# Separate load buffers for modulation chunks, their products three weight steps behind the load, and a written-out order on the load queue and on VectorE

## The chip, the core and the metric

The kernel runs on one core of a Trainium2 chip. The metric is device time in microseconds (us), the median of three runs. Engines are named as in the profile: PE is TensorE (PEld its weight loads), DVE is VectorE, ACT is ScalarE, POOL is GpSimd, and SP is the sync engine, which here does nothing but issue loads and stores.

## What is computed

Two layers of a diffusion transformer on 256 tokens of width 2048, in fp32. Layer 0 mixes tokens with a Hyena long convolution, layer 1 with a short gated convolution, and each ends in a SwiGLU feed-forward part of width 5632. Every sub-layer is modulated by vectors that come from one conditioning vector `c`:

```
m = silu(c) @ w_mod + b_mod            # six vectors of 2048 for each layer
sh1, sc1, g1, sh2, sc2, g2 = split(m)
a = rmsnorm(x, norm1_g) * (1 + sc1) + sh1
x = x + g1 * mixer(a)                  # hyena: w_in 2048x6144, w_out 2048x2048; short conv alike
a = rmsnorm(x, norm2_g) * (1 + sc2) + sh2
x = x + g2 * (silu(a @ w_gate) * (a @ w_up)) @ w_down
out = rmsnorm(x, final_g)
```

`w_mod` is 2 x 2048 x 12288 in fp32, some 200 MB of the 620 MB that the kernel reads. The rest are the weights of the matmuls.

## The kernel before

**Weights.** All matmul weights pass through one stream of 784 chunks of 128 x 1024 fp32 (512 KB). `emit_chunk(i)` loads chunk i into a tile `wraw`, and `split` makes two float32r tiles of it: ACT casts it to `whi` (L207), DVE subtracts that from the raw chunk and gives `wlo` (L208). `whi` and `wlo` have four buffers each. `lin` calls `next_chunk` once for two k tiles (one weight step); the chunks are emitted three steps ahead of the matmuls that use them (`LA = 3`). A step is 24 matmuls of 256 columns, or, where both parts of the activations lie side by side (`wide`), 8 of 512 columns (L258) and 8 of 256 (L262).

**Modulation.** The product `silu(c) @ w_mod` is not done on PE. Its weights come as 384 more chunks of 512 KB, tiles `mraw`; for each, one DVE instruction (L191) multiplies the chunk by the broadcast `cb` and sums along its rows into a column of `macc`. When a block of four k tiles is complete, `mod_finish` makes `mval` (L162, L163) and, for scales, `msc` (L166) of it. `mod_list` is the order of the chunks, `emit_mods(n)` takes the next n of them, each with its load and its product. Each segment of the program has a rate `mods`, in modulation chunks for each weight step, which `emit_chunk` adds up in `credit`: 0.9 in the hyena output and in the first feed-forward parts, 0.58 (`MF0`) in the rest of the feed-forward part of layer 0, 0.6 (`ML1`) in most of the short convolution, 0.2 in the last feed-forward part. `need_mods(l, m, kb)` takes as many as are missing before a modulation vector is read.

**Buffers and order.** `wraw` and `mraw` share one pool, `rawp`, of seven buffers. All loads are issued on SP, which takes them in order: a load whose buffer is not yet free holds up those behind it. The order of the instructions on each engine is not the order of the source: the program is built with a scheduler that simulates a timeline (`schedule_with_timeline_sim=True`) and places instructions by it. DVE, too, takes its instructions in that order and waits at the first one that isn't ready.

**Entries.** `Entry` begins a sub-layer before its norm is known: `prep` scales the residual and splits it (`xs`, `xsh`, `xsl`) and needs the shift vector for that, two groups of matmuls run on it, and then `make_a` makes the activations `ax`: DVE scales (`an`, L350), ACT adds the shift (L353), DVE gives the low part (L354). `make_a` needs both `msc` and `mval`. The layers' second norms have the keys `n2_0` and `n2_1`.

Of the kernel before, what the change touches and what calls it, by code (L numbers as in the profile page):

```python
# [11 lines left out]
F32 = mybir.dt.float32  # L12
# [3 lines left out]
ALU = mybir.AluOpType  # L16

P = 128
D = 2048
KT = D // P  # L20
T = 256
# [8 lines left out]
KD = 8  # L30
# [7 lines left out]
HT, HD, HI = 1, 1, 4  # L38
XW = T + 2

RSQRT_MAGIC = float(0x5F3759DF)
# [15 lines left out]


class Seg:
    def __init__(self, fn, chunks=(), mods=0.0):  # L60
# [4 lines left out]
def trunk_kernel(ctx: ExitStack, tc: tile.TileContext, A, out):  # L65
    nc = tc.nc

    cst = ctx.enter_context(tc.tile_pool(name="cst", bufs=1))
    rawp = ctx.enter_context(tc.tile_pool(name="rawp", bufs=7))
    hilo = ctx.enter_context(tc.tile_pool(name="hilo", bufs=4))  # L70
# [5 lines left out]
    def nm(s):  # L76
        uid[0] += 1
        return f"{s}_{uid[0]}"
# [12 lines left out]

# [1 line left out]
    crow = []  # L93
# [22 lines left out]
    def load_cols():  # L116
        nc.sync.dma_start(out=dcol, in_=A["k_dcol"])
        nc.sync.dma_start(out=vec, in_=A["vecs"])

    def V(name, i=0, n=1):  # L120
# [29 lines left out]

# [1 line left out]
    macc, mval, msc = {}, {}, {}  # L152
# [29 lines left out]

    def emit_mods(n):
        for _ in range(n):
            if mod_pos[0] >= len(mod_list):
                return
            l, m, kt, h, fin = mod_list[mod_pos[0]]
            mod_pos[0] += 1
            r = rawp.tile([P, 1024], F32, tag="raw", name=nm("mraw"))
            nc.sync.dma_start(out=r, in_=A["wm"][l, m, kt, h])  # L190
            nc.vector.scalar_tensor_tensor(  # L191
                out=r, in0=r, scalar=1.0, in1=cb[:, h * 1024:(h + 1) * 1024],
                op0=ALU.mult, op1=ALU.mult, accum_out=macc[l, m][:, kt, h:h + 1])
            if fin:
                mod_finish(l, m, *fin)

    def mods_through(n):
        emit_mods(max(0, n - mod_pos[0]))

    mod_end = {(e[0], e[1], e[2] // 4): i + 1 for i, e in enumerate(mod_list)}  # L200
# [3 lines left out]

# [1 line left out]
    def split(dst_hi, dst_lo, src):  # L206
        nc.scalar.copy(out=dst_hi, in_=src)  # L207
        nc.vector.tensor_tensor(out=dst_lo, in0=src, in1=dst_hi.bitcast(F32), op=ALU.subtract)  # L208

    stream, spos, semit, ready = [], [0], [0], {}  # L210
    LA = 3
    credit = [0.0]

    def emit_chunk(i):
        ap, mods = stream[i]
        r = rawp.tile([P, 1024], F32, tag="raw", name=nm("wraw"))
        nc.sync.dma_start(out=r, in_=ap)
        hi = hilo.tile([P, 1024], F32R, tag="hi", name=nm("whi"))
        lo = hilo.tile([P, 1024], F32R, tag="lo", name=nm("wlo"), bufs=NLO)
        split(hi, lo, r)  # L220
        ready[i] = (hi, lo)
        credit[0] += mods
        n = int(credit[0])
        credit[0] -= n
        emit_mods(n)
# [7 lines left out]
    def next_chunk():  # L233
        i = spos[0]
        spos[0] += 1
        while semit[0] < min(i + LA + 1, len(stream)):
            emit_chunk(semit[0])
            semit[0] += 1
        if bg:
            bg.pop(0)()  # L240
        return ready.pop(i)
# [21 lines left out]

# [1 line left out]
    def rsqrt_steps(v, y, a, b):  # L265
# [15 lines left out]
    def rstd_from(parts):  # L281
        # parts: tiles [P, n, T] of squares, summed over partitions with tokens on partitions
        p = ps("pss")
        for h in range(2):
            cols = [t[:, j, h * P:(h + 1) * P] for t in parts for j in range(t.shape[1])]
            for i, c in enumerate(cols):
                nc.tensor.matmul(p[:, h:h + 1], c, ones[:, 0:1], start=(i == 0), stop=(i == len(cols) - 1))
        return rstd_of([p[:, 0:2]])
# [40 lines left out]
    def pairs(n, name):  # L329
        # [part, k tile, hi/lo, token]: both parts of a k tile lie side by side  # L330
        ts = [S([P, 2, 2, T], F32R, name) for _ in range(n // 2)]
# [24 lines left out]

# [1 line left out]
    def sin_layer(w, rhs, bcol, n):  # L358
# [102 lines left out]

    def a_task(kb):
        make_a(acts0, kb, x0[kb], st0["r"], 0, True)

# [18 lines left out]

# [1 line left out]
    segs = []  # L485
# [3 lines left out]

# [1 line left out]
    a0 = acts0  # L491
# [168 lines left out]
    class Entry:  # L660
# [44 lines left out]
        def group(self, i, order):  # L705
            # groups 0 and 1 over the first KD k tiles, before the statistics are known
            flush_bg()
# [134 lines left out]

# [1 line left out]
    e1 = Entry(1, True, "n1_1")  # L844
# [71 lines left out]
    def tail_close(pss):  # L916
        # the last four feature tiles enter the sum of squares one by one
        p = acc_box["tail"]
# [31 lines left out]

# [1 line left out]
def _chunks(w):  # L952
# [80 lines left out]
```

## Time and profile before

| | us |
|---|---|
| median of 3 runs | 2444.77 (2442.78 to 2445.31) |
| span of the profiled execution, first to last instruction | 2440.7 |
| median less that span | 4.1 |
| PE busy in the span | 2363.8 |
| DVE busy | 1848.5 |
| ACT busy | 1119.7 |

The profiled execution is known by its span alone; the 4.1 us are the difference of two executions and are taken as what lies around the span. A matmul counts as busy from its start to a modelled end, so PE's share says little: how many matmuls start in a stretch is the better measure. A waiting engine is shown with what released it.

### The profile page before, as it was taken

How to read it: one execution, taken by the hardware profiler on the slowest of the kernel's cores; microseconds unless marked ns; L12 is line 12 of the kernel's file. 1: busy time of each engine (PE TensorE's matmuls, PEld its weight loads, DVE VectorE, ACT ScalarE, POOL GpSimd, SP SyncE). 2: the span in 40 equal slices, each digit the busy share in tenths (PEclk: the TensorE clock that was granted, in tenths of full speed). 3: DMA queues.
4: the chain of work that ended last, by engine and by line, in shares of the span. 5: the costliest groups of instructions: out<-in, count | busy, mean ns of one | idle time of the engine just before them, and what ended most of it. 6: DMA issues, size and time to landing. Idle time of an engine off the chain costs nothing.

```text
span 2440.7 us, 38816 instructions
## 1 busy us (share of the span) xinstructions
PE 2363.8 (97%) x15040; PEld 2111.2 (87%) x15040; DVE 1848.5 (76%) x2729; ACT 1119.7 (46%) x1527; POOL 83.2 (3%) x94
## 2 busy tenths in 40 slices
PE   7899999999999999999999999999999999999998
PEld 3699998999998888888789888879988888888887
DVE  7979999898887777777777988778766656655554
ACT  3445444454544333444345444435545433444543
POOL 5000111010000000000000000001000000000000
PEclk9899999999999999999999999999999999999998
DMA  7899776889888888888876888886777677755662
GB/s 268 319 333 329 244 225 209 293 316 333 314 283 276 281 283 278 273 289 278 275 260 195 300 306 285 273 264 222 234 220 228 222 221 228 232 184 188 186 185 95
DMA packets 172525, 624.24 MB, mean 256 GB/s; under 512 B 19533, under 2 KB 19886, under 8 KB 172340
## 3 DMA queue, kind: packets, MB, share of 16 engines
q1 hardware_dynamic: 172340, 621.77, 76.5%
q8 instruction: 117, 1.92, 0.3%
q14 instruction: 68, 0.56, 0.1%
HBM read 619.59 MB, written 2.10 MB: 255 GB/s over the span
## 4 chain that ended last, share of the span: by engine, by line
PE 70%; DMA 14%; DVE 10%; issue 4%; POOL 1%; ACT 0%; DVEq 0%; SPq 0%; ACTq 0%; POOLq 0%
PE ps L258 26%; PE ps L262 23%; DMA mraw<-in_wm 14%; PE ps L261 9%; PE ps L260 9%; DVE wlo L208 4%; DVE mraw L191 3%; DVE xres L753 1%; DVE fy L368 0%; POOL rs L277 0%; DVE cg L342 0%; PE pz L616 0%; PE pz L615 0%; PE pz L617 0%; PE pU L583 0%
## 5 line engine op out<-in xcount | busy, mean ns | idle before, releaser
L207 ACT CAST whi<-wraw 128x1024 fp32r<-128x1024 f32 x784 | 816.3, 1049 | 932.0 <-PE ps L258 625.3
L208 DVE TENSOR_TENSOR wlo<-wraw,whi 128x1024 fp32r<-128x1024 f32 x784 | 950.3, 1220 | 298.8 <-ACT whi L207 298.1
L262 PE MATMUL ps<-ax,wlo 128*128 128x256 f32 x4160 | 1138.5, 283 | 15.0 <-DVE wlo L208 14.6
L258 PE MATMUL ps<-ax,whi 128*128 128x512 f32 x2688 | 945.6, 398 | 0.0
L262 PEld LDWEIGHTS ps<-ax,wlo 128*128 128x128 f32 x4160 | 780.7, 191 | 27.6 <-DVE wlo L208 23.6
L191 DVE SCALAR_TENSOR_TENSOR mraw<-mraw,cb 128x1024 f32<-128x1024 f32 x384 | 477.6, 1246 | 245.8 <-DMA mraw<-in_wm 245.5
L258 PEld LDWEIGHTS ps<-ax,whi 128*128 128x128 f32 x2688 | 504.0, 188 | 118.6
L258 PE MATMUL ps<-hx,whi 128*128 128x512 f32 x1328 | 468.2, 397 | 0.0
L261 PE MATMUL ps<-ax,whi 128*128 128x256 f32 x1472 | 409.7, 285 | 1.8 <-DVE ax L354 1.8
L260 PE MATMUL ps<-ax,whi 128*128 128x256 f32 x1472 | 404.0, 285 | 7.5 <-ACT whi L207 5.7
L262 PE MATMUL ps<-hx,wlo 128*128 128x256 f32 x1408 | 397.2, 282 | 9.5 <-DVE wlo L208 9.3
L258 PEld LDWEIGHTS ps<-hx,whi 128*128 128x128 f32 x1328 | 249.3, 188 | 59.6
L260 PEld LDWEIGHTS ps<-ax,whi 128*128 128x128 f32 x1472 | 281.7, 194 | 8.8 <-ACT whi L207 6.5
L261 PEld LDWEIGHTS ps<-ax,whi 128*128 128x128 f32 x1472 | 284.9, 194 | 2.3 <-DVE ax L354 2.0
L262 PEld LDWEIGHTS ps<-hx,wlo 128*128 128x128 f32 x1408 | 266.2, 189 | 14.7 <-DVE wlo L208 14.4
L262 PE MATMUL ps<-zx,wlo 128*128 128x256 f32 x512 | 143.0, 284 | 6.2 <-DVE wlo L208 5.9
L262 PEld LDWEIGHTS ps<-zx,wlo 128*128 128x128 f32 x512 | 96.5, 190 | 9.6 <-DVE wlo L208 9.6
L341 ACT COPY fb<-ps 128x256 f32<-128x256 f32 x168 | 61.8, 369 | 91.5 <-DVE cg L342 59.8
L258 PE MATMUL ps<-zx,whi 128*128 128x512 f32 x256 | 90.9, 398 | 0.0
L753 DVE SCALAR_TENSOR_TENSOR xres<-ps,mval,xres 128x256 f32<-128x256 f32 x168 | 72.4, 476 | 12.3 <-PE ps L262 12.1
L260 PE MATMUL ps<-zx,whi 128*128 128x256 f32 x256 | 71.2, 283 | 0.7 <-DVE z L619 0.7
L261 PE MATMUL ps<-zx,whi 128*128 128x256 f32 x256 | 71.7, 283 | 0.0
(153 smaller groups left out, 1598.5 us busy)
## 6 DMA issues: line engine op xcount, KB each, us to landing
mraw<-in_wm SPq DMA_DIRECT2D x384, 512.0 KB, 4.7
wraw<-in_wgu SPq DMA_DIRECT2D x352, 512.0 KB, 4.5
wraw<-in_wd SPq DMA_DIRECT2D x176, 512.0 KB, 4.3
wraw<-in_hw_in SPq DMA_DIRECT2D x96, 512.0 KB, 5.0
wraw<-in_sw_in SPq DMA_DIRECT2D x96, 512.0 KB, 4.4
wraw<-in_hw_out SPq DMA_DIRECT2D x32, 512.0 KB, 5.0
wraw<-in_sw_out SPq DMA_DIRECT2D x32, 512.0 KB, 4.4
xin<-in_xT SPq DMA_DIRECT2D x4, 512.0 KB
```

Of the source, the lines that this page charges most:

```text
L191: nc.vector.scalar_tensor_tensor(out=r, in0=r, scalar=1.0, in1=cb[:, h * 1024:(h + 1) * 1024], op0=ALU.mult, op1=ALU.mult, accum_out=macc[ ...
L207: nc.scalar.copy(out=dst_hi, in_=src)
L208: nc.vector.tensor_tensor(out=dst_lo, in0=src, in1=dst_hi.bitcast(F32), op=ALU.subtract)
L258: nc.tensor.matmul(pss[n], wh, both, start=st, stop=False)
L260: nc.tensor.matmul(o, wh, xh, start=st, stop=False)
L261: nc.tensor.matmul(o, wh, xl, start=False, stop=False)
L262: nc.tensor.matmul(o, wl, xh, start=False, stop=sp)
L341: nc.scalar.copy(out=b, in_=p[:, T:2 * T])
L753: nc.vector.scalar_tensor_tensor(out=xa, in0=pss[n][:, c * T:(c + 1) * T], scalar=mval[l, gate][:, kt:kt + 1], in1=xa, op0=ALU.mult, op1=A ...
```

## The change

The pool `rawp` has five buffers instead of seven and holds weight chunks (and one table, `draw`). A new pool `mrawp` has five buffers for modulation chunks. The load of a modulation chunk and its product are parted: `load_mods` issues the load and puts the product into a list `mq`; `drain_mods` takes products off it that are three calls of `next_chunk` old (`MLAG`), and a full list (five) or a `need_mods` takes them earlier. `emit_chunk` first issues the loads of chunks up to i + 2 (`RL`) and then splits chunk i. `chain` ties each instruction that it is given to the one before it with the same key, without a semaphore: it fixes their order for the scheduler. There is one such chain of all `wraw` and `mraw` loads on SP, and one of all `wlo` subtractions and modulation products on DVE. What else is on DVE is still placed by the scheduler. `a_task` asks for its modulation vectors itself. The program reserves less memory for dynamic DMA (`dynamic_dma_scratch_size=1024`), and some comments are gone.

```diff
+RAWB, MRAWB, MLAG, RL = 5, 5, 3, 2
+NOSYNC = mybir.DependencyInfo(mybir.DependencyClass.NoSync, mybir.DependencyReason.DATA)
-    rawp = ctx.enter_context(tc.tile_pool(name="rawp", bufs=7))
+    rawp = ctx.enter_context(tc.tile_pool(name="rawp", bufs=RAWB))
+    mrawp = ctx.enter_context(tc.tile_pool(name="mrawp", bufs=MRAWB))
+    def chain(key, ins):
+        p = last.get(key)
+        if p is not None:
+            tc.add_manual_dep(ins.ins, p.ins.name, NOSYNC, reason="chain")
+        last[key] = ins
+        return ins
-    def emit_mods(n):
+    def run_mod(r, l, m, kt, h, fin):
+        chain("dve", nc.vector.scalar_tensor_tensor(
+            out=r, in0=r, scalar=1.0, in1=cb[:, h * 1024:(h + 1) * 1024],
+            op0=ALU.mult, op1=ALU.mult, accum_out=macc[l, m][:, kt, h:h + 1]))
+        if fin:
+            mod_finish(l, m, *fin)
+    def drain_mods(upto):
+        while mq and mq[0][0] <= upto:
+            mq.pop(0)[1]()
+    def load_mods(n):
         for _ in range(n):
             if mod_pos[0] >= len(mod_list):
                 return
-            l, m, kt, h, fin = mod_list[mod_pos[0]]
+            e = mod_list[mod_pos[0]]
             mod_pos[0] += 1
-            r = rawp.tile([P, 1024], F32, tag="raw", name=nm("mraw"))
-            nc.sync.dma_start(out=r, in_=A["wm"][l, m, kt, h])
-            nc.vector.scalar_tensor_tensor(
-                out=r, in0=r, scalar=1.0, in1=cb[:, h * 1024:(h + 1) * 1024],
-                op0=ALU.mult, op1=ALU.mult, accum_out=macc[l, m][:, kt, h:h + 1])
-            if fin:
-                mod_finish(l, m, *fin)
+            if len(mq) >= MRAWB:
+                mq.pop(0)[1]()
+            r = mrawp.tile([P, 1024], F32, tag="mraw", name=nm("mraw"))
+            chain("sp", nc.sync.dma_start(out=r, in_=A["wm"][e[0], e[1], e[2], e[3]]))
+            mq.append((mtick[0], lambda r=r, e=e: run_mod(r, *e)))
+    def emit_mods(n):
+        load_mods(n)
     def mods_through(n):
         emit_mods(max(0, n - mod_pos[0]))
+        while mod_pos[0] - len(mq) < n:
+            mq.pop(0)[1]()
+    def load_raw(i):
+        r = rawp.tile([P, 1024], F32, tag="raw", name=nm("wraw"))
+        chain("sp", nc.sync.dma_start(out=r, in_=stream[i][0]))
+        raws[i] = r
     def emit_chunk(i):
-        ap, mods = stream[i]
-        r = rawp.tile([P, 1024], F32, tag="raw", name=nm("wraw"))
-        nc.sync.dma_start(out=r, in_=ap)
+        mods = stream[i][1]
+        while lpos[0] < min(i + RL + 1, len(stream)):
+            load_raw(lpos[0])
+            lpos[0] += 1
+        r = raws.pop(i)
...
-        split(hi, lo, r)
+        chain("dve", split(hi, lo, r))
...
             emit_chunk(semit[0])
             semit[0] += 1
+            mtick[0] += 1
+            drain_mods(mtick[0] - MLAG)
...
     def a_task(kb):
+        need_mods(0, 0, kb)
         make_a(acts0, kb, x0[kb], st0["r"], 0, True)
...
-    nc = bacc.Bacc("TRN2", target_bir_lowering=False, num_devices=1)
+    nc = bacc.Bacc("TRN2", target_bir_lowering=False, num_devices=1, dynamic_dma_scratch_size=1024)
```

What this does to the order of the instructions is shown at three places. A name's last number counts the tiles in the source's order, so a load and its reader carry the same number.

The first place is the feed-forward part of layer 0, in the down projection. On SP before, the loads stand in this order:

```order
L217 DMA wraw_10080<-in_wd 128x1024
L190 DMA mraw_10086<-in_wm 128x1024
L217 DMA wraw_10105<-in_wd 128x1024
L217 DMA wraw_10127<-in_wd 128x1024
L190 DMA mraw_10133<-in_wm 128x1024
L217 DMA wraw_10152<-in_wd 128x1024
L190 DMA mraw_10158<-in_wm 128x1024
```

On DVE before, the readers of these loads stand like this:

```order
L208 TENSOR_TENSOR wlo_10061<-wraw_10058,whi_10060 128x1024
L191 SCALAR_TENSOR_TENSOR mraw_10158,macc_1_123<-mraw_10158,cb 128x1024
L208 TENSOR_TENSOR wlo_10083<-wraw_10080,whi_10082 128x1024
L208 TENSOR_TENSOR wlo_10108<-wraw_10105,whi_10107 128x1024
L191 SCALAR_TENSOR_TENSOR mraw_10217,macc_1_123<-mraw_10217,cb 128x1024
L208 TENSOR_TENSOR wlo_10130<-wraw_10127,whi_10129 128x1024
L208 TENSOR_TENSOR wlo_10155<-wraw_10152,whi_10154 128x1024
```

The product of `mraw_10158` stands ahead of the splits of four weight chunks (10080, 10105, 10127, 10152) that are loaded before it. Over the whole feed-forward part of layer 0, every product stands four splits ahead in this way (five in one case).

The loads of the same part on SP now:

```order
L249 DMA wraw_10016<-in_wd 128x1024
L249 DMA wraw_10039<-in_wd 128x1024
L220 DMA mraw_10045<-in_wm 128x1024
L249 DMA wraw_10064<-in_wd 128x1024
L249 DMA wraw_10086<-in_wd 128x1024
L220 DMA mraw_10092<-in_wm 128x1024
```

And their readers on DVE now:

```order
L239 TENSOR_TENSOR wlo_10067<-wraw_10016,whi_10066 128x1024
L239 TENSOR_TENSOR wlo_10089<-wraw_10039,whi_10088 128x1024
L201 SCALAR_TENSOR_TENSOR mraw_10045,macc_1_126<-mraw_10045,cb 128x1024
L239 TENSOR_TENSOR wlo_10114<-wraw_10064,whi_10113 128x1024
L239 TENSOR_TENSOR wlo_10136<-wraw_10086,whi_10135 128x1024
L201 SCALAR_TENSOR_TENSOR mraw_10092,macc_1_126<-mraw_10092,cb 128x1024
```

Now the readers stand in the order of the loads; so it is everywhere but at 17 products at the end of the hyena output, at the entry `n2_1` and in the first down projection of layer 1, which stand one or two splits ahead.

The second place is the end of the hyena output, where `prep` of `n2_0` takes the modulation chunks that are missing. DVE before, from one split to the third after it:

```order
L208 TENSOR_TENSOR wlo_5564<-wraw_5561,whi_5563 128x1024
L678 COPY xs_5570<-mval_3_115 128x3x2
L191 SCALAR_TENSOR_TENSOR mraw_5615,macc_3_114<-mraw_5615,cb 128x1024
L319 TENSOR_TENSOR sqh_5554<-sq_5552 128x512
L191 SCALAR_TENSOR_TENSOR mraw_5618,macc_3_114<-mraw_5618,cb 128x1024
L191 SCALAR_TENSOR_TENSOR mraw_5621,macc_3_114<-mraw_5621,cb 128x1024
L208 TENSOR_TENSOR wlo_5606<-wraw_5603,whi_5605 128x1024
L208 TENSOR_TENSOR xsl_5576<-xs_5570,xsh_5575 128x774
L324 TENSOR_TENSOR ssacc_4987<-ssacc_4987,sqh_5554 128x512
L191 SCALAR_TENSOR_TENSOR mraw_5624,macc_3_114<-mraw_5624,cb 128x1024
L208 TENSOR_TENSOR wlo_5665<-wraw_5662,whi_5664 128x1024
```

DVE now, in the same weight step, up to the next split (two products, `mraw_5517` and `mraw_5569`, and `sqh_5556` stand just ahead of the first row, behind `wlo_5611`):

```order
L177 TENSOR_TENSOR mval_4_120<-macc_4_119 128x4
L239 TENSOR_TENSOR xsl_5581<-xs_5575,xsh_5580 128x774
L201 SCALAR_TENSOR_TENSOR mraw_5614,macc_3_117<-mraw_5614,cb 128x1024
L366 TENSOR_TENSOR ssacc_4993<-ssacc_4993,sqh_5556 128x512
L178 TENSOR_TENSOR mval_4_120<-mval_4_120,vec 128x4
L201 SCALAR_TENSOR_TENSOR mraw_5617,macc_3_117<-mraw_5617,cb 128x1024
L201 SCALAR_TENSOR_TENSOR mraw_5619,macc_3_117<-mraw_5619,cb 128x1024
L181 SCALAR_TENSOR_TENSOR msc_4_121<-mval_4_120,vec 128x4
L201 SCALAR_TENSOR_TENSOR mraw_5621,macc_3_117<-mraw_5621,cb 128x1024
L201 SCALAR_TENSOR_TENSOR mraw_5624,macc_3_117<-mraw_5624,cb 128x1024
L201 SCALAR_TENSOR_TENSOR mraw_5627,macc_3_117<-mraw_5627,cb 128x1024
L239 TENSOR_TENSOR wlo_5672<-wraw_5563,whi_5671 128x1024
```

Between two splits there were at most three products; now there are eight in a row, with `sqh`, `xsl` and `ssacc` among them, before `wlo_5672`.

The third place is the entry `n2_1`, where the first two activation blocks are made. The activations of k tiles 12 and 13 are `ax_17685` before and `ax_17692` now; chunk 530 of the stream (counted from 0) is multiplied by them. On DVE before, they stand behind split 530 (`wlo_17763`):

```order
L208 TENSOR_TENSOR wlo_17714<-wraw_17711,whi_17713 128x1024
L354 SCALAR_TENSOR_TENSOR ax_17683<-an_17720,mval_3_129,ax_17683 128x256
L354 SCALAR_TENSOR_TENSOR ax_17683<-an_17724,mval_3_129,ax_17683 128x256
L354 SCALAR_TENSOR_TENSOR ax_17684<-an_17728,mval_3_129,ax_17684 128x256
L354 SCALAR_TENSOR_TENSOR ax_17684<-an_17732,mval_3_129,ax_17684 128x256
L208 TENSOR_TENSOR wlo_17763<-wraw_17760,whi_17762 128x1024
L354 SCALAR_TENSOR_TENSOR ax_17685<-an_17780,mval_3_129,ax_17685 128x256
```

Now the last five products of the shift vector and four `an` stand behind split 530 (`wlo_17769`), and the rows that follow are these (`wlo_17938` is split 533):

```order
L201 SCALAR_TENSOR_TENSOR mraw_17778,macc_3_131<-mraw_17778,cb 128x1024
L392 SCALAR_TENSOR_TENSOR an_17799<-xres_4645,msc_4_135,rstd_17684 128x256
L392 SCALAR_TENSOR_TENSOR an_17849<-xres_4639,msc_4_135,rstd_17684 128x256
L392 SCALAR_TENSOR_TENSOR an_17853<-xres_4639,msc_4_135,rstd_17684 128x256
L239 TENSOR_TENSOR wlo_17846<-wraw_17718,whi_17845 128x1024
L239 TENSOR_TENSOR wlo_17892<-wraw_17766,whi_17891 128x1024
L239 TENSOR_TENSOR wlo_17938<-wraw_17843,whi_17937 128x1024
L177 TENSOR_TENSOR mval_3_132<-macc_3_131 128x4
L178 TENSOR_TENSOR mval_3_132<-mval_3_132,vec 128x4
L396 SCALAR_TENSOR_TENSOR ax_17692<-an_17787,mval_3_132,ax_17692 128x256
```

The activations that chunk 530 needs moved from behind split 530 to behind split 533, and split 533 needs the buffer of chunk 529.

## Rows read from the trace of the kernel before

**Rows 1.** The page: span, and busy time of each engine.
```profile
span 2440.7 us, 38816 instructions
...
PE 2363.8 (97%) x15040; PEld 2111.2 (87%) x15040; DVE 1848.5 (76%) x2729; ACT 1119.7 (46%) x1527; POOL 83.2 (3%) x94
```

**Rows 2.** Stretches: from:to, length, busy us (count) per engine, clock, DMA share, GB/s.
```profile
120.00:240.00 120.00, 120.00 (x1002) 120.00 (x1002) 103.23 (x157) 60.52 (x85) 0.00 (x0) 1.00 0.93 330
...
480.00:520.00 40.00, 40.00 (x335) 40.00 (x335) 38.07 (x61) 20.46 (x25) 0.00 (x0) 1.00 0.97 353
...
780.00:1260.00 480.00, 461.53 (x2576) 394.88 (x2575) 352.86 (x513) 199.29 (x244) 0.00 (x0) 1.00 0.84 279
1520.00:1660.00 140.00, 132.70 (x732) 111.65 (x732) 106.74 (x162) 58.06 (x73) 0.00 (x0) 1.00 0.81 266
...
1800.00:2340.00 540.00, 540.00 (x3058) 468.20 (x3057) 319.05 (x402) 244.33 (x311) 0.00 (x0) 1.00 0.67 211
```

**Rows 3.** Waits in 780 to 1260: total us, times, longest us.
```profile
DVE mraw L191 <- DMA mraw<-in_wm: 126.8, 80, 3.5
...
PE ps L262 <- DVE wlo L208: 18.1, 26, 1.8
```

**Rows 4.** DVE in order of time, 1103 to 1110: start, us, what, idle before.
```profile
1103.37 1.23 DVE L191 SCALAR_TENSOR_TENSOR mraw<-mraw,cb 128x1024 f32<-128x1024 f32 x1 [0.73 <-DMA mraw<-in_wm]
...
1104.52 2.36 DVE L208 TENSOR_TENSOR wlo<-wraw,whi 128x1024 fp32r<-128x1024 f32 x2
1109.43 1.22 DVE L191 SCALAR_TENSOR_TENSOR mraw<-mraw,cb 128x1024 f32<-128x1024 f32 x1 [2.56 <-DMA mraw<-in_wm]
```

**Rows 5.** SP in order of time, the load for that second product.
```profile
1104.63 0.33 SPq L190 DMA_DIRECT2D mraw<-in_wm  x1
```

**Rows 6.** The page's costliest groups: the two halves of a split.
```profile
L207 ACT CAST whi<-wraw 128x1024 fp32r<-128x1024 f32 x784 | 816.3, 1049 | 932.0 <-PE ps L258 625.3
L208 DVE TENSOR_TENSOR wlo<-wraw,whi 128x1024 fp32r<-128x1024 f32 x784 | 950.3, 1220 | 298.8 <-ACT whi L207 298.1
```

**Rows 7.** DVE in order of time, late in the hyena input (369 to 392).
```profile
369.64 2.35 DVE L208 TENSOR_TENSOR wlo<-wraw,whi 128x1024 fp32r<-128x1024 f32 x2
371.91 0.68 DVE L594 TENSOR_TENSOR ym<-pU,Kspec 128x512 f32<-128x512 f32 x1
...
377.49 2.31 DVE L191 SCALAR_TENSOR_TENSOR mraw<-mraw,cb 128x1024 f32<-128x1024 f32 x1
...
391.52 1.21 DVE L208 TENSOR_TENSOR wlo<-wraw,whi 128x1024 fp32r<-128x1024 f32 x1
```

**Rows 8.** PE in order of time, its waits at 392 and 441.
```profile
392.79 0.39 PE L262 MATMUL ps<-ax,wlo 128*128 128x256 f32 x1 [3.54 <-DVE wlo L208]
...
441.39 0.74 PE L617 MATMUL pz<-mh,Yl 128*128 128x256 f32 x4 [1.65 <-DVE Yl L208]
442.87 0.38 PE L260 MATMUL ps<-zx,whi 128*128 128x256 f32 x1 [0.74 <-DVE z L619]
```

**Rows 9.** Two stretches of 10 us around 400, columns as in rows 2.
```profile
390.00:400.00 10.00, 7.21 (x48) 7.21 (x49) 10.00 (x15) 2.23 (x3) 0.66 (x1) 0.83 0.59 172
400.00:410.00 10.00, 10.00 (x87) 10.00 (x86) 8.85 (x15) 5.51 (x9) 0.00 (x0) 1.00 0.90 315
```

**Rows 10.** DVE and then PE in order of time, entry n2_0.
```profile
541.89 1.27 DVE L350 SCALAR_TENSOR_TENSOR an<-xres,msc,rstd 128x256 f32<-128x256 f32 x3
...
544.22 1.22 DVE L191 SCALAR_TENSOR_TENSOR mraw<-mraw,cb 128x1024 f32<-128x1024 f32 x1
...
545.89 0.39 PE L261 MATMUL ps<-ax,whi 128*128 128x256 f32 x1 [1.77 <-DVE ax L354]
```

**Rows 11.** DVE at startup, first and last of ten products in a row.
```profile
75.22 1.21 DVE L191 SCALAR_TENSOR_TENSOR mraw<-mraw,cb 128x1024 f32<-128x1024 f32 x1
...
85.75 1.21 DVE L191 SCALAR_TENSOR_TENSOR mraw<-mraw,cb 128x1024 f32<-128x1024 f32 x1
```

**Rows 12.** The page's DMA issues: count, KB each, median us to landing.
```profile
mraw<-in_wm SPq DMA_DIRECT2D x384, 512.0 KB, 4.7
```

More of the change, by code (lines that the diff above doesn't have):

```diff
@@ L118, in load_cols @@
         nc.sync.dma_start(out=vec, in_=A["vecs"])
+    last = {}
+    def chain(key, ins):
[4 more added lines that the diff above has]
+        return ins
     def V(name, i=0, n=1):
@@ L181, in trunk_kernel @@
     mod_pos = [0]
-    def emit_mods(n):
+    mq, mtick = [], [0]
+    def run_mod(r, l, m, kt, h, fin):
[8 more added lines that the diff above has]
+    def load_mods(n):
         for _ in range(n):
@@ L207, in split @@
         nc.scalar.copy(out=dst_hi, in_=src)
-        nc.vector.tensor_tensor(out=dst_lo, in0=src, in1=dst_hi.bitcast(F32), op=ALU.subtract)
+        return nc.vector.tensor_tensor(out=dst_lo, in0=src, in1=dst_hi.bitcast(F32), op=ALU.subtract)
     stream, spos, semit, ready = [], [0], [0], {}
@@ L212, in trunk_kernel @@
     credit = [0.0]
-    def emit_chunk(i):
-        ap, mods = stream[i]
-        r = rawp.tile([P, 1024], F32, tag="raw", name=nm("wraw"))
-        nc.sync.dma_start(out=r, in_=ap)
+    raws, lpos = {}, [0]
+    def load_raw(i):
+        r = rawp.tile([P, 1024], F32, tag="raw", name=nm("wraw"))
+        chain("sp", nc.sync.dma_start(out=r, in_=stream[i][0]))
+        raws[i] = r
+    def emit_chunk(i):
+        mods = stream[i][1]
[3 more added lines that the diff above has]
+        r = raws.pop(i)
         hi = hilo.tile([P, 1024], F32R, tag="hi", name=nm("whi"))
         lo = hilo.tile([P, 1024], F32R, tag="lo", name=nm("wlo"), bufs=NLO)
-        split(hi, lo, r)
+        chain("dve", split(hi, lo, r))
         ready[i] = (hi, lo)
```

## The prediction

> **What bounds the kernel now.** First the page's first lines: PE counts as busy for 2363.8 of 2440.7 us [rows 1]. Since a busy PE is not PE at its peak, I then cut the span into stretches and counted the matmuls that start in each. Where only 256-column matmuls run, 1002 start in 120 us, 0.1198 us each; where wide steps run undisturbed, 3058 start in 540 us, 0.1766 each in their mix [rows 2]. A weight step is thus 24 x 0.1198 = 2.88 us narrow, or 16 x 0.1766 = 2.83 us wide. Most of the span runs at that pace and can give nothing. Two wide stretches don't: 780 to 1260, the bulk of layer 0's feed-forward part, has 2576 matmuls, worth 2576 x 0.1766 = 454.9 us, in 480, so 25.1 us are lost; 1520 to 1660, the short convolution, has 732, worth 129.3 in 140, so 10.7 are lost [rows 2]. The clock is full in both. PE's own waits there come to only 18.1 us in 26 pieces; the rest of the loss hides in the modelled ends of matmuls.
>
> Next, who is late in 780 to 1260: PE waits for `wlo` and DVE waits for loads of `mraw`, 126.8 us in 80 waits [rows 3]. The order of instructions (the first place above) says how: a product stands four splits ahead of weights that were loaded before it. DVE in order of time shows one round. The product at 1103.37 ends at 1104.60, splits follow, and the next product starts at 1109.43 after 2.56 us of waiting [rows 4]. Its load was issued at 1104.63, just as the earlier product had ended [rows 5], 4.8 us before its use; a load of `mraw` takes 4.7 us in the median [rows 12]. So each product frees the buffer that the next product's load needs, DVE sits out a whole trip of a load, and the splits behind the waiting product come late for PE. It is not lack of bandwidth as such: the DMA share is 0.84 at 279 GB/s, while 480 to 520 shows 353 GB/s with PE at its own pace, 335 x 0.1198 = 40.1 us in 40 [rows 2].
>
> **The change part by part.** The sum is made against the profiled execution, 2440.7, plus the 4.1 us by which the median lies above it [rows 1].
>
> *Feed-forward part of layer 0.* With products in load order and five weight buffers, weight load j can be issued when split j-5 is done, and the `mraw` load behind it at the same time, since its own five buffers are freed far earlier. Both are then about five steps, 5 x 2.83 = 14.1 us, ahead of their readers; three times the 4.7 us of a trip. DVE has 352.86 us of work for 454.9 us of PE [rows 2, 3]; 78%, so it keeps up if the pieces come evenly: between two splits stands at most one product, 1.2 + 1.2 us in 2.83. The traffic would be 279 x 480/454.9 = 294 GB/s, below the 353 shown. Bounds: 0 to -25.1. I take **-25.1**, being nearest to the undisturbed stretch.
>
> *Short convolution.* The same pattern (products four splits ahead) and the same bounds, 0 to -10.7; 266 x 140/129.3 = 288 GB/s. I take **-10.7**.
>
> *Hyena input.* Between the splits at 369.64 and 391.52 DVE has some 19 us of other work, among it three products, one of 2.31 us [rows 7] and two of 1.2. PE waits 3.54 us for the late split at 392.79 [rows 8] and then runs at a granted clock of 0.83: 48 matmuls in 7.21 us where 48 x 0.1198 = 5.75 would do, 1.5 lost [rows 9]. In the new order these three products stand elsewhere, 4.7 us less before the split, which covers the 3.54. Both losses go: **-5** (0 to -8; beyond -5 if the waits around it shrink too). Just behind it PE waits 1.65 for `Yl` and 0.74 for `z` [rows 8]; `Yl` stands earlier now: **-2** (0 to -3).
>
> *End of the hyena output, `n2_0`.* This is the second place. PE's cover: a split can start when the step four before it has freed its `hi`/`lo` buffers, and its halves take 1.05 + 1.22 = 2.3 us [rows 6]; so what stands between two splits, the later split's own 1.2 included, is hidden up to 4 x 2.88 - 2.3 = 9.2 us. There stand eight products at 1.15 = 9.2 us (ten in a row at startup start 1.17 apart [rows 11]), `sqh` and `ssacc` at about 0.6 each (`ym` of that width 0.68 [rows 7]) and `xsl` about 0.9 (between `ym` and a product by its width), 11.5 with small change, 12.7 with the split. Stall 3.5, and behind a stall of that length a stretch at reduced clock as after the 3.54 above, 1.5. One product, 1.22 us, leaves the chain at 544.22 ahead of PE's wait of 1.77 [rows 10]: -1.2. Net **+4** (0 if the scheduler's order leaves `hi`/`lo` slack that I don't see; 8 if the loads of these eight, for five buffers, come late too). Queued behind the products is `wlo_5672`, for which only PE waits.
>
> *Entry `n2_1`.* The third place. The activations for chunk 530 now stand behind split 533. That split needs the buffer of chunk 529, so PE finishes 529 and then has nothing until split 533 and the `ax` rows are through: ACT's and DVE's halves 2.3, then `mval`, the `ax` of k tile 12 (0.42 each, as `an` [rows 10]) with ACT's adds between. But DVE itself comes late: five products 5.8, four `an` 1.7, three splits 3.6 stand in the row, 11 us before `mval`. I take a wait of 5 and 1.5 of clock: **+6.5** (3, the bare chain behind 529, to 9, with DVE's row half uncovered).
>
> *Startup.* Ten products come 1.17 us apart [rows 11]: by the buffers, five allow a round of 4.7 + 1.15 = 5.9 us, 1.17 each, just the present pace. By bandwidth 0.524 MB at 353 GB/s is 1.49 us [rows 2]. So **+1** (-0.5 to +2). *At no cost:* a cluster of six products in the first down projection of layer 1, 6.9 us, lies under the cover of 4 x 2.83 - 2.3 = 9.0 (gone, the excess over it would show on PE); the reserved DMA memory issues nothing; the ties carry no semaphore.
>
> Sum: -25.1 - 10.7 - 5 - 2 + 4 + 6.5 + 1 = -31.3; 2440.7 - 31.3 + 4.1 = 2413.5, forecast **2414 us**.
>
> **A rule against it.** [Rows 2] show 353 GB/s in 480 to 520, in loads of 512 KB. The Trainium skill, "DMA: Bandwidth & Descriptors", section "Measured (HBM→SBUF, 128 partitions, SWDGE, issued from GpSimd)", asks to batch transfers to 1 MiB or more for three quarters of the peak and lists 341 GB/s at 1 MB; by it 512 KB loads would be near their limit, and an earlier issue would buy little: rival 3's time. The trace disagrees, by those 353 GB/s.
>
> **Rivals.** 1. *The two entries don't stall:* what I count as late in the written order is covered by slack on ACT and PE. For it: covers of 9 us exist; against it: the present order has waits of 3.54 and 1.77 at lighter places [rows 8, 10]. Without +4 and +6.5, 2403 us. 2. *Half of the feed-forward gain:* DVE at 78% becomes the pacer, since pieces of `swiglu` and of the norm fall between split and product, which are now bound to one order. 25.1 + 10.7 half recovered: 2414 + 18 = 2432. 3. *The loads are at their limit, slower:* if the mix of weights and modulation can't be had faster than the 279 GB/s of 780 to 1260, the loss there moves from "product waits" to "split waits" and nothing of 35.8 comes back, while the entries and startup still cost 11.5 and the hyena gives 7: 2444.8 + 4.5 = 2449. It decides from the point where less than 4.5 of 35.8 us are recovered, that is if the stretch stays below some 282 GB/s (an eighth of the way from 279 to 294, and a little). Against it: 353, and 330 over 120 to 240 [rows 2]. 4. *It doesn't do what it says:* PE's lost time there has another source, since its waits for `wlo` are only 18.1 of 25.1 us [rows 3], and the clumps cost less than I think: about 2445.
>
> **How the numbers follow.** Forecast with its sizes 58%, its own range 2405 to 2423; rival 1 17%; rival 2 14%; rival 3 6%; rival 4 5%. A measurement of this kernel tells some 0.2%, 4.9 us, from no change. The first three cases all lie below 2440: faster 0.89; rival 4 gives same 0.05; rival 3 slower 0.06. The range 2399 to 2435 holds the first three down to a rival 1 with 4 us more of hyena and up to a rival 2 with 3 us less; left out are rivals 3 and 4, 11%, and the tails of the others, some 6%.
>
> **What would show it.** Right: the feed-forward stretch with about 342 matmuls for each 60 us (60/0.1766 = 340) and DMA near 294 GB/s; DVE's waits for `mraw` there from 126.8 us to a few; the 3.54 before the hyena's convolution gone; new PE waits of about 3.5 us behind `wlo_5672` and 5 us for `ax` at `n2_1`. Wrong: DVE waiting for `wraw` instead at an unchanged rate (rival 3); PE waits for `wlo` while DVE is never idle (rival 2); no new waits at the entries (rival 1); startup longer by more than 2 us.

## The result, and the profile after

The changed kernel takes **2405.28 us** (median; 2404.43 to 2406.43) against 2445.04 for the kernel before, run beside it: a ratio of 0.9842, 95% interval 0.9828 to 0.9856. The forecast was 2414 with a range of 2399 to 2435. The profiled execution has a span of 2402.6, 2.7 below the median; the span fell by 38.1 us.

The top of the page of the changed kernel, to be read against [rows 1]:

```profile
span 2402.6 us, 38382 instructions
...
PE 2344.8 (98%) x15040; PEld 2107.5 (88%) x15040; DVE 1851.5 (77%) x2729; ACT 1125.3 (47%) x1527; POOL 75.1 (3%) x94
...
mraw<-in_wm SPq DMA_DIRECT2D x384, 512.0 KB, 5.5
```

Each engine has as many working instructions as before, and a load of `mraw` takes longer to land, 5.5 us against 4.7 [rows 12]. So no load became faster; what went is waiting. Stretches of the changed kernel, columns as in [rows 2]:

```profile
505.00:515.00 10.00, 6.76 (x44) 6.55 (x44) 9.41 (x15) 3.48 (x4) 0.00 (x0) 0.83 0.99 362
...
1660.00:1670.00 10.00, 4.04 (x34) 3.84 (x32) 10.00 (x17) 2.10 (x2) 0.00 (x0) 0.83 0.32 93
1670.00:1680.00 10.00, 8.86 (x53) 8.86 (x54) 9.39 (x22) 7.31 (x21) 0.00 (x0) 0.66 0.47 190
...
780.00:1260.00 480.00, 480.00 (x2719) 416.19 (x2718) 372.78 (x534) 215.71 (x261) 0.00 (x0) 1.00 0.84 288
```

In 780 to 1260 now 2719 matmuls start, 0.1765 us each: PE's own pace, as forecast (480 / 0.1766 = 2718, or 340 in 60 us; the 342 beside it in the prediction is a slip). The three longest waits there:

```profile
ACT whi L238 <- PE ps L300: 250.8, 164, 1.8
DVE wlo L239 <- ACT whi L238: 98.7, 117, 1.6
DVE xres L796 <- PE ps L304: 7.2, 7, 1.4
```

The 126.8 us of DVE waiting for `mraw` [rows 3] have no row any more. DVE waits for ACT, and ACT for PE to free a `whi` buffer: PE sets the pace. DVE in order of time shows the same place as [rows 4]:

```profile
1101.27 1.22 DVE L201 SCALAR_TENSOR_TENSOR mraw<-mraw,cb 128x1024 f32<-128x1024 f32 x1
...
1102.95 1.23 DVE L239 TENSOR_TENSOR wlo<-wraw,whi 128x1024 fp32r<-128x1024 f32 x1 [0.46 <-ACT whi L238]
1105.82 1.23 DVE L239 TENSOR_TENSOR wlo<-wraw,whi 128x1024 fp32r<-128x1024 f32 x1 [1.64 <-ACT whi L238]
1106.96 1.22 DVE L201 SCALAR_TENSOR_TENSOR mraw<-mraw,cb 128x1024 f32<-128x1024 f32 x1
```

No product carries a wait. The two stalls that were forecast stand in the trace. First the clump at the end of the hyena output, the eight products in a row, on DVE (the rows between are left out):

```profile
495.15 1.21 DVE L239 TENSOR_TENSOR wlo<-wraw,whi 128x1024 fp32r<-128x1024 f32 x1
496.29 1.22 DVE L201 SCALAR_TENSOR_TENSOR mraw<-mraw,cb 128x1024 f32<-128x1024 f32 x1
...
505.46 1.22 DVE L201 SCALAR_TENSOR_TENSOR mraw<-mraw,cb 128x1024 f32<-128x1024 f32 x1
...
507.24 1.23 DVE L201 SCALAR_TENSOR_TENSOR mraw<-mraw,cb 128x1024 f32<-128x1024 f32 x1 [0.56 <-DMA mraw<-in_wm]
...
508.39 3.49 DVE L239 TENSOR_TENSOR wlo<-wraw,whi 128x1024 fp32r<-128x1024 f32 x3
```

and PE behind it:

```profile
509.66 0.58 PE L304 MATMUL ps<-zx,wlo 128*128 128x256 f32 x1 [3.24 <-DVE wlo L239]
```

From 496.29 to the end of the late split some 13 us, as worked out; PE waits 3.24. Then the entry `n2_1`, on DVE:

```profile
1659.48 1.22 DVE L201 SCALAR_TENSOR_TENSOR mraw<-mraw,cb 128x1024 f32<-128x1024 f32 x1
...
1664.46 1.22 DVE L201 SCALAR_TENSOR_TENSOR mraw<-mraw,cb 128x1024 f32<-128x1024 f32 x1
...
1666.80 3.49 DVE L239 TENSOR_TENSOR wlo<-wraw,whi 128x1024 fp32r<-128x1024 f32 x3
1670.20 0.15 DVE L177 TENSOR_TENSOR mval<-macc 128x4 f32<-128x4 f32 x1
```

and on PE, which waits for the activation that needs that `mval`:

```profile
1671.14 1.23 PE L302 MATMUL ps<-ax,whi 128*128 128x256 f32 x4 [7.10 <-ACT ax L395]
```

Where the time went is seen best by setting the start of the n-th matmul of one trace against that of the other (both issue 15040, in nearly the same order; worked out from the starts in the traces, us):

```
n-th matmul   before    after   after - before   what lies since the row above
 1200          220.1    221.7    +1.6            startup
 3200          480.4    476.5    -3.9            hyena input, its convolution
 3600          528.4    529.4    +1.0            clump at n2_0
 4000          581.4    577.5    -3.9            entry n2_0
 5600          782.5    779.2    -3.3            first part of layer 0's feed-forward
 8400         1301.7   1273.1   -28.6            the rest of it
 9600         1491.7   1462.2   -29.5
10700         1689.7   1649.1   -40.6            short convolution and its output
10800         1703.7   1661.2   -42.4            a wait for rdiag at n2_1 that is gone
11200         1764.8   1732.4   -32.4            entry n2_1
12800         2047.5   2015.0   -32.4
14800         2399.3   2361.3   -38.1            down projections of layer 1
```

### The profile page after: what moved, and what is told of

Same layout as the page of the kernel before. It is cut to its first block, busy times and chain, and to the rows that moved or that the text cites. A ratio compares the mean times of both kernels' runs of the same rounds, so it can differ in the third digit from the quotient of the medians.

```text
span 2402.6 us, 38382 instructions
## 1 busy us (share of the span) xinstructions
PE 2344.8 (98%) x15040; PEld 2107.5 (88%) x15040; DVE 1851.5 (77%) x2729; ACT 1125.3 (47%) x1527; POOL 75.1 (3%) x94
## 4 chain that ended last, share of the span: by engine, by line
PE 93%; DVE 5%; DMA 1%; issue 1%; POOL 1%; ACT 0%; SPq 0%; DVEq 0%; ACTq 0%; POOLq 0%
PE ps L300 42%; PE ps L304 30%; PE ps L302 9%; PE ps L303 9%; DVE mraw L201 2%; DVE wlo L239 1%; DVE fy L410 0%; DMA wraw<-in_hw_in 0%; DMA wraw<-in_wgu 0%; DVE kfil L482 0%; PE pz L659 0%; PE pz L660 0%; PE pz L658 0%; DMA mraw<-in_wm 0%; DVE ax L396 0%
## 5 line engine op out<-in xcount | busy, mean ns | idle before, releaser
L304 PE MATMUL ps<-ax,wlo 128*128 128x256 f32 x4160 | 1155.1, 281 | 0.0
L201 DVE SCALAR_TENSOR_TENSOR mraw<-mraw,cb 128x1024 f32<-128x1024 f32 x384 | 471.7, 1232 | 1.3 <-DMA mraw<-in_wm 1.1
L302 PE MATMUL ps<-ax,whi 128*128 128x256 f32 x1472 | 411.4, 285 | 20.0 <-ACT whi L238 11.0
L303 PE MATMUL ps<-ax,whi 128*128 128x256 f32 x1472 | 414.7, 284 | 1.5 <-DVE ax L396 1.5
```

Source lines behind the costliest of these rows:

```text
L201: chain("dve", nc.vector.scalar_tensor_tensor(out=r, in0=r, scalar=1.0, in1=cb[:, h * 1024:(h + 1) * 1024], op0=ALU.mult, op1=ALU.mult, ac ...
L302: nc.tensor.matmul(o, wh, xh, start=st, stop=False)
L303: nc.tensor.matmul(o, wh, xl, start=False, stop=False)
L304: nc.tensor.matmul(o, wl, xh, start=False, stop=sp)
```

## The experiments

Four theories were set against each other. **A:** a product costs time when its load is issued less than a trip ahead of it, and the order of the readers is what sets that lead. **B:** the product's place ahead of the splits costs, whatever its lead. **C:** the separate pools are what helps. **D:** the lag and the early weight loads carry part of it. Each run was timed beside the kernel before, whose medians lie between 2442.45 and 2445.04 us on these occasions, so a difference of under 3 us between two variants says nothing by itself.

**The written-out order alone.** To the kernel before, only `chain` was added, at its three places:

```diff
-            nc.sync.dma_start(out=r, in_=A["wm"][l, m, kt, h])
-            nc.vector.scalar_tensor_tensor(
+            chain("sp", nc.sync.dma_start(out=r, in_=A["wm"][l, m, kt, h]))
+            chain("dve", nc.vector.scalar_tensor_tensor(
...
-        nc.sync.dma_start(out=r, in_=ap)
+        chain("sp", nc.sync.dma_start(out=r, in_=ap))
...
-        split(hi, lo, r)
+        chain("dve", split(hi, lo, r))
```

> The kernel before with nothing added but the two written-out orders (loads on SP; splits and products on DVE): seven shared buffers, load and product issued together, weights loaded when they are split. Every product then stands in the order of the loads. Theory A: the order alone gives the lead (seven buffers freed in load order, 12.5 us), so layer 0's feed-forward part and the short convolution run at PE's pace and the time is that of the changed kernel, 2400 to 2410. Theory D: the earlier weight loads and the lag of the products carry part of the gain; 2415 to 2445.

Measured 2399.65 us, 0.9823 (0.9809 to 0.9838) of before. The stretch 780 to 1260 has 2719 matmuls, as in the changed kernel, and DVE's longest waits there are for ACT, none for `mraw`:

```profile
780.00:1260.00 480.00, 480.00 (x2719) 416.17 (x2718) 371.63 (x532) 216.06 (x261) 0.00 (x0) 1.00 0.84 289
...
DVE wlo L220 <- ACT whi L219: 104.4, 120, 1.7
```

The order brings the whole gain; D falls. Of the two orders it is that of DVE: a program built with the tie on the loads taken out too (it was not run) has the same rows on SP, DVE and PE, so here that tie changes nothing.

**One shared pool of seven**, the rest as changed (at most three products pending).

```diff
-RAWB, MRAWB, MLAG, RL = 5, 5, 3, 2
+RAWB, MRAWB, MLAG, RL = 7, 3, 3, 2
-    mrawp = ctx.enter_context(tc.tile_pool(name="mrawp", bufs=MRAWB))
-            r = mrawp.tile([P, 1024], F32, tag="mraw", name=nm("mraw"))
+            r = rawp.tile([P, 1024], F32, tag="raw", name=nm("mraw"))
```

> The changed kernel with one pool of seven buffers for both kinds of chunks, as before, and the written-out order kept. Theory A (a product loses time when its load is issued less than a load's trip ahead of it): seven buffers, freed in the order in which they are loaded, are 7 / 1.58 loads for each step = 4.4 steps or 12.5 us of lead against a trip of 4.7, so nothing waits and the time stays at 2405 within 5 us. Theory C (the separate pools are what helps): products wait again in layer 0's feed-forward part and the short convolution, 36 us come back, about 2441.

2402.62 us, 0.984 (0.9813 to 0.9867), and 2719 matmuls in the stretch. C falls from this side.

**The pools alone**, on the kernel before, without order and lag.

```diff
-    rawp = ctx.enter_context(tc.tile_pool(name="rawp", bufs=7))
+    rawp = ctx.enter_context(tc.tile_pool(name="rawp", bufs=5))
+    mrawp = ctx.enter_context(tc.tile_pool(name="mrawp", bufs=5))
...
-            r = rawp.tile([P, 1024], F32, tag="raw", name=nm("mraw"))
+            r = mrawp.tile([P, 1024], F32, tag="mraw", name=nm("mraw"))
...
-    nc = bacc.Bacc("TRN2", target_bir_lowering=False, num_devices=1)
+    nc = bacc.Bacc("TRN2", target_bir_lowering=False, num_devices=1, dynamic_dma_scratch_size=1024)
```

> The kernel before with the two pools of five buffers and nothing else: no written-out order, no lag. The scheduler now takes modulation chunks as early as buffers allow: 90 of them stand between weight chunks 50 and 100, where the changed kernel has 27, and all 384 by chunk 300. Theory: without the order the pools don't give the gain. In the hyena input, where DVE is busy for 96% of the time (115.45 of 120 us), 63 more products of 1.22 us are 77 us of DVE work that nothing covers; against it stand the 36 us won back where no product is left: 2460 to 2490. Rival: the pools alone free the loads, about 2405.

2495.96 us, slower, 1.0221 (1.0204 to 1.0238). The stretch in the hyena input shows why; DVE is busy without a gap:

```profile
240.00:480.00 240.00, 191.52 (x1341) 184.54 (x1339) 240.00 (x420) 86.16 (x123) 20.34 (x12) 0.87 0.86 303
```

By the 2800th matmul this kernel is 81 us behind the one before; 77 were worked out. C falls from the other side too: freed from the shared buffers, the scheduler runs the products into the stretch that has no room on DVE.

**The lag at nought.**

```diff
-RAWB, MRAWB, MLAG, RL = 5, 5, 3, 2
+RAWB, MRAWB, MLAG, RL = 5, 5, 0, 2
```

> Product issued right behind its load instead of three steps later; five and five buffers. Every product then stands two splits ahead of weights that were loaded before it. Theory A: weight load n is issued when split n-5 is done, the product runs behind split n-2, so the lead is three steps, 8.5 us, more than the trip: 2405 within 5 us, next to no DVE waits for modulation loads. Theory B (a product's place ahead of the splits costs, whatever its lead): half of the depth of before, half of the 36 us come back, about 2423.

2403.83 us, 0.9844 (0.9822 to 0.9867). All products stand two splits ahead, and in 780 to 1260 it costs nothing:

```profile
780.00:1260.00 480.00, 480.00 (x2719) 416.26 (x2718) 372.71 (x535) 216.63 (x262) 0.00 (x0) 1.00 0.83 288
```

No product waits for its load there, so B falls. Up to the 4000th matmul this kernel is 4.6 us behind the changed one, and it wins that back in layer 1, most of it at the faster matmul pace in the short convolution (last section); so the equal times are in part chance.

**The same order, a lead of two steps** (four weight buffers).

```diff
-RAWB, MRAWB, MLAG, RL = 5, 5, 3, 2
+RAWB, MRAWB, MLAG, RL = 4, 5, 0, 2
```

> Between the two runs with lag 0: four weight buffers. The order of the readers is as there, every product two splits ahead; weight load n is issued when split n-4 is done, the lead is two steps, 5.7 us. Theory A (lead against trip): as in the run without the order on DVE, whose lead is also two steps though its products stand three splits ahead: 2410 to 2425. Theory B (place alone): as with five buffers, 2404.

2425.03 us, 0.9924 (0.9905 to 0.9942), the upper end of A. The profiled execution is the fastest of the four, with a span of 2415.8; what the slower three lost besides (6 to 8 us), no trace shows. **No order on DVE**, five and five buffers, also a lead of two steps:

```diff
-        chain("dve", nc.vector.scalar_tensor_tensor(
+        (nc.vector.scalar_tensor_tensor(
...
-        chain("dve", split(hi, lo, r))
+        split(hi, lo, r)
```

> The changed kernel without the written-out order on DVE; that of the loads stays. The scheduler then puts each product three splits ahead of weights that were loaded before it. Theory A: lead of two steps, 5.7 us, just above the median trip: some short waits of DVE, little lost on PE, 2405 to 2412. Theory B: three quarters of the 36 us come back, about 2432. In both, the rows of products and splits at the two norm entries are the scheduler's again, so the wait of 3.5 us at the end of the hyena output may go.

2418.09 us, 0.9901 (0.9878 to 0.9925): between A's 2412 and B's 2432. Of the 12.6 us by which its span is above the changed kernel's, 5.7 are the slower matmul pace in layer 1's down projections (last section), which neither theory had. The wait for the late split at the hyena output's end is gone, as said, though PE then waits 1.9 us for `xsl` and 2.2 for `ax`. At `n2_1` it still waits 5.8 us for `ax`, without any order on DVE. These two runs, seen together, sharpen A. DVE's waits in 780 to 1260, with the stretch itself, for four weight buffers:

```profile
DVE mraw L201 <- DMA mraw<-in_wm: 92.9, 72, 3.5
...
780.00:1260.00 480.00, 480.00 (x2719) 416.30 (x2718) 370.53 (x534) 211.64 (x256) 0.00 (x0) 1.00 0.83 290
```

and without the order on DVE:

```profile
DVE mraw L201 <- DMA mraw<-in_wm: 113.7, 76, 3.7
...
780.00:1260.00 480.00, 474.48 (x2685) 410.37 (x2684) 364.33 (x530) 208.08 (x255) 0.00 (x0) 1.00 0.84 287
```

The first waits 92.9 us and PE loses nothing here: busy and waiting together are 370.5 + 92.9 = 463 of 480, so DVE still has time over. The second comes to 364.3 + 113.7 = 478 and loses 480 - 2685 x 0.1766 = 5.9 us. The kernel before comes to 352.9 + 126.8 = 479.7 [rows 2, 3] and loses 25.1. In these three, waits for loads are free until they use up DVE's idle time; from there PE pays. The waits of the products follow the lead: none at three steps, 92.9 and 113.7 us at two. What the first of the two loses, it loses elsewhere: in the first part of the feed-forward, where products come 0.9 to a step, 7 us (matmuls 4400 to 4800), and in the hyena, 6 us against the changed kernel by the 3200th matmul. Its four buffers make the weights late as well, and longer in sum than the products, in 580 to 700:

```profile
ACT whi L238 <- DMA wraw<-in_wgu: 28.9, 17, 3.3
DVE mraw L201 <- DMA mraw<-in_wm: 22.1, 19, 4.0
```

So its time does not show what the lead of the products alone costs; the waits in 780 to 1260, where no weight is waited for, do show that a shorter lead makes them wait.

**Three weight buffers**, the order as with lag 0.

```diff
-RAWB, MRAWB, MLAG, RL = 5, 5, 3, 2
+RAWB, MRAWB, MLAG, RL = 3, 5, 0, 2
```

> As the run with lag 0, with three weight buffers instead of five. The order of the readers is the same as there, but weight load n is now issued when split n-3 is done and the product stands behind split n-2: a lead of one step, 2.8 us, less than the trip. Theory A: each of some 80 products in 480 us of layer 0's feed-forward part waits about 2 us, DVE needs 1.72 x 1.22 + 1.23 + 2 = 5.3 us for a cycle of 4.88, PE falls back by 8%, some 35 us there and 40 to 60 us in all: 2445 to 2465. Theory B: the same as with five buffers.

2793.71 us, 1.1432 (1.1393 to 1.147): the direction of A, but eight times its size. The waits in 780 to 1260 tell why it isn't a clean test:

```profile
ACT whi L238 <- DMA wraw<-in_wgu: 167.9, 78, 4.9
DVE mraw L201 <- DMA mraw<-in_wm: 159.5, 63, 5.1
ACT whi L238 <- DMA wraw<-in_wd: 109.9, 42, 4.2
```

The products wait 2.5 us each, about the 2 expected, but the weights themselves arrive late as well, which A had not counted.

**Rates that dissolve the clumps.**

```diff
-HM = 0.55
-HMO = 0.9
+HM = 0.6
+HMO = 1.0
-MF0, MA, ML0, ML1 = 0.58, 0.9, 0.2, 0.6
+MF0, MA, ML0, ML1 = 0.58, 0.9, 0.2, 0.65
```

> The changed kernel with three rates changed: hyena input 0.55 to 0.60, hyena output 0.9 to 1.0, short convolution and its output 0.6 to 0.65, so that the modulation chunks of both second norms are loaded in time and the entries take none in a clump (three products instead of eight before the late split at n2_0, none instead of five at n2_1). Theory: PE's waits of 3.5 us at n2_0 and 7.4 us at n2_1 come from the clumps; both go, with what the clock loses behind them, 10 to 14 us, to 2391 to 2396. Rival: at n2_1 the wait stays because the scale and add of the activation blocks are placed late whatever the products do: 2400. Second rival: two loads in each step of the hyena output (364 GB/s) are more than the queue gives, and 3 to 9 us are lost there.

2400.93 us, 0.9831 (0.9816 to 0.9845); short of the 2391 to 2396. At `n2_1` no wait of PE is left, and the 10 us that the changed kernel loses from the 10800th to the 11200th matmul are not lost (-42.2 at both against before). So that stall came from the clump of products, and not from the order on DVE as such, without which it stood too (5.8 us above). The wait of 3.24 at `n2_0` went as well, but with the extra products in the hyena input this kernel is 6.6 us behind the changed one by the 3200th matmul, more than that wait. The 5.7 us that the changed kernel wins in layer 1's down projections are not won here, by what the next two runs are about.

**Another order of the wide matmuls:** two of 512 columns, then two of 256, for each output tile; then all eight and all eight. The edit of the first is shown; in the second the new `if wide` block has a loop over all output tiles of its own, ahead of the other.

```diff
             for n in range(G):
+                if wide:
+                    for kk in range(2):
+                        c0 = kk * 512 + n * P
+                        nc.tensor.matmul(pss[n], hi[:, c0:c0 + P], xs[kk][2], start=start and kc == k0 and kk == 0, stop=False)
                 for kk in range(2):
...
-                    if wide:
-                        nc.tensor.matmul(pss[n], wh, both, start=st, stop=False)
-                    else:
+                    if not wide:
```

> The changed kernel with another order of the wide matmuls: for each tile of outputs two of 512 columns, then two of 256, instead of one and one in turn. The same work. In the changed kernel's trace three pairs take either 1.06 or 1.04 us for hundreds of us on end, whatever DVE and the loads do. If the two paces belong to the strict alternation of 512 and 256, another order leaves it: at 1.04 for all, 1112 us at the slow pace become 1091, 2384. If not, 2405.

> As the run before, with all eight matmuls of 512 columns of a step first and then all eight of 256. At the pace of the narrow stretches (32 columns' time over the width for each matmul) a step takes 8 x 0.227 + 8 x 0.120 = 2.77 us instead of 2.83: 2384 if the alternation makes the slow pace, 2405 if not.

2390.6 us, 0.9788 (0.9774 to 0.9803), and 2393.68 us, 0.9803 (0.9786 to 0.9819). Both beat the changed kernel, by 14.7 and 11.6 us; not by all of the 21 expected, since the pace now is one between the two (below).

**Together:** the order alone, the short convolution's rate at 0.65, the wide matmuls two and two. The edit is those of the first run, of the run with two and two, and `ML1` of the rates.

> The kernel before with the written-out orders alone, the short convolution's modulation rate at 0.65 instead of 0.6, and the wide matmuls two and two. From 2399.65: no clump at n2_1, so its wait of 7.4 us and what the clock loses behind it go, -10; each wide step 2.787 us instead of a mix of 2.773 and 2.827, -9 or so: 2378 to 2384.

2379.66 us, 0.9744 (0.9729 to 0.9758): the best of all, 25.6 us below the changed kernel, without its pools, its lag or its early loads.

## Why the prediction was right, and where it was off

**The feed-forward part** is where the argument was, and it held in kind and size: -25.1 forecast, -25.3 measured (matmuls 5600 to 8400). The traffic there is 288 GB/s (294 worked out). The **short convolution** gave 11.1 for 10.7 (matmuls 9600 to 10700). That it is the order of the readers that gives the lead, and not the new buffers, the prediction did not separate; the runs did.

**The hyena input** gave -5.5 from startup's end to its own (-7 forecast): the wait of 3.54 [rows 8] is gone, which gave 5.3 where 5 was forecast. The -2 for `Yl` and `z` failed: `Yl` is no longer waited for, but the wait for `z` grew from 0.74 to 2.48 us, and 0.2 was won there. **Startup** cost 1.6 (1 forecast).

**`n2_0`** is a term whose stall was right and whose net was wrong. The stall is 3.24 us, and with what the clock costs behind it (granted 0.83 in the mean of 505 to 515) it is +4.9 in all; 3.5 and 1.5 were forecast. But the prediction took back only one product of 1.2 us at the entry, and the entry gave back all 4.9: the waits of 1.8 for `ax` and 1.1 for `rdiag` that PE had there don't occur. With the order alone, whose clump is six products, PE doesn't wait at the clump (0.3 us) and waits 3.0 us for `ax` at the entry, and both kernels stand 4 us ahead of before at the 4000th matmul. The stall only stands at another place: as far as these two show, what DVE has to do up to the entry is the bound, and the sum should have had 0 there, not +4.

**`n2_1`** is the step that failed in size: +6.5 forecast with bounds of 3 and 9, +10.0 measured. The row of DVE was counted rightly, 11 us from the first product to `mval` (1659.48 to 1670.20), but "I take a wait of 5" let some half of it be covered. PE had finished its last ready step at 1664.0, 4.5 us into the row, so 7.1 were left. The mean granted clock is 0.66 in 1670 to 1680, and what lies behind the wait cost 2.9, not 1.5. Just ahead of it the entry gave 1.8 back that the sum did not have: before, PE waited 1.55 us for `rdiag` there.

**Not in the sum:** those 1.8, 5.7 us in layer 1's down projections, where nothing that the change moved was late, and 1.4 us outside the span (2.7 where 4.1 was taken). The prediction held that wide steps at 0.1766 us for each matmul "can give nothing"; the down projections ran at 0.1731 (last section). With the -4 at `n2_0` these come to -12.9; the 3.5 more at `n2_1` and 1.5 less in the hyena input take 5 of them back, which leaves most of the 8 us by which the time came out below the sum of 2413.5. That the total lies so near is thus in part luck: `n2_1` came out beyond its bounds, and errors of both signs cancelled.

**The rivals.** The entries did stall, so rival 1 is wrong, though its time of 2403 came close, for other reasons. Rivals 2 and 4 are ruled out by the 2719 matmuls and by the missing waits. Rival 3, loads at their limit, is ruled out by the same stretch. The kernel before had shown more than the 353 GB/s that the prediction set against it:

```profile
100.00:110.00 10.00, 10.00 (x86) 10.00 (x85) 8.80 (x13) 5.89 (x8) 0.00 (x0) 1.00 1.01 400
```

The Trainium skill, "DMA: Bandwidth & Descriptors", section "Measured (HBM→SBUF, 128 partitions, SWDGE, issued from GpSimd)", gives 341 GB/s for transfers of 1 MB and asks to batch to 1 MiB or more. That table is for loads issued from GpSimd; the loads here are issued on SP, have half the size and reached these 400 GB/s, eight of them issued in the 10 us, so the measurement decides.

## What to carry to other kernels

When one queue feeds two kinds of readers on one engine, let the engine read in the order in which the queue loads: a reader that stands far ahead of older loads (four splits here; two cost nothing with five weight buffers) turns its own buffer's release into the next load's start, and the engine sits out the trip. Add the engine's busy time and its waits for loads in a stretch: in the runs here the waits cost PE time only where the sum came near the whole stretch. And more buffers do not replace the order (alone they made this kernel 2.2% slower). Work that falls due at a point, as at the entries, should be spread by its rate ahead of the point, into a stretch in which the engine has room.

## What the runs showed of the hardware

The wide steps ran at two paces with nothing waiting. Two stretches of the changed kernel, both at full clock, alternating 512 and 256 columns:

```profile
1800.00:2050.00 250.00, 250.00 (x1417) 216.79 (x1416) 152.92 (x193) 107.84 (x130) 0.00 (x0) 1.00 0.71 228
2070.00:2320.00 250.00, 250.00 (x1444) 218.54 (x1443) 140.36 (x170) 123.04 (x166) 0.00 (x0) 1.00 0.62 190
```

0.1764 and 0.1731 us for each matmul. By the starts in the trace, three pairs take 1.060 or 1.040 us, and the pace holds for hundreds of us: some 1112 us at the slow one and 355 at the fast one in the changed kernel. It changes there where the order of the matmuls is broken for a moment, as here, four of 512 in a row on PE:

```profile
2060.97 0.40 PE L300 MATMUL ps<-ax,whi 128*128 128x512 f32 x1
2061.20 0.28 PE L304 MATMUL ps<-ax,wlo 128*128 128x256 f32 x1
2061.32 1.11 PE L300 MATMUL ps<-ax,whi 128*128 128x512 f32 x4
```

The variant with one shared pool changes at the same matmul the other way, from fast to slow, so the break chooses no side; the kernel before runs on at the slow pace, and that is the 5.7 us. In the kernel before, the pace changes at PE's waits too: 1.060 us ahead of a wait of 1.22 us at 846.36, 1.040 behind it, and 1.060 again behind one of 1.41 us at 881.55. So it ran some 194 of the 480 us of 780 to 1260 at the faster pace, worth an estimated 194 x 0.020 / 1.04 = 3.7 us, and the 25.1 us lost there are what was left of a loss of some 29. With two and two in turn the same stretches are alike:

```profile
1800.00:2050.00 250.00, 250.00 (x1437) 218.09 (x1436) 158.55 (x202) 107.89 (x125) 0.00 (x0) 1.00 0.70 232
2070.00:2320.00 250.00, 250.00 (x1437) 218.16 (x1436) 140.24 (x171) 119.63 (x158) 0.00 (x0) 1.00 0.60 189
```

0.1740 us each. Why an alternation has two paces, and what picks one, stays open; differences of up to 6 us among the variants of this study can come from it alone. Of the 4.8 us by which the span of the order alone is shorter than the changed kernel's, 3.2 arise at the faster pace in the short convolution (matmuls 9600 to 10800).
